# One hybrid attention and recurrence block on one core: high weights meet both token parts in one product, gate scaling on ScalarE, and two streams of work change places

## The chip, the cores and the metric

The kernel runs on one core of a Trainium2 chip. The metric is device time in microseconds (us). The kernel before takes 1622.03 us, the median of three runs between 1621.97 and 1623.56 us. Engines are named as in the profile: PE is TensorE's matmul, PEld its weight load, DVE is VectorE, ACT is ScalarE, POOL is GpSimd and SP is SyncE, which issues most DMAs.

## The reference, cut to what matters

All of it is fp32: 256 tokens and 256 context tokens of width 2048, one layer. `att`, `hgrn2_bidir`, `readout` and `rope` stand for the window attention with a sink, the gated two-way recurrence over 16 heads, its normed and gated output and the rotary embedding.

```python
mod = silu(c) @ w_ada + b_ada                       # 2048 -> 3 x 2048
shift, scale, gate = split(mod, 3)                  # the same for the context, without gate
xn = rmsnorm(x) * (1 + scale) + shift               # and cn from ctx
aq, ak, av, ag, hq, hff, hfb, hi, hg, ma, mb = split_columns(xn @ w_in)   # 19456 columns
att_branch = att(rope(aq), rope(ak), av, ctx keys and values) * silu(ag)
f = lb + (1 - lb) * sigmoid(hff)                    # forget gates, also for hfb and for the context
o = hgrn2_bidir(silu(hq), hi, 1 - f, log f, ...)    # starts from states of the context
hg_branch = readout(o) * silu(hg)                   # silu(hg): the "output gate"
y = sigmoid(ma + b0) * (hg_branch @ w_o_hgrn) + sigmoid(mb + b1) * (att_branch @ w_o_attn)
out = rmsnorm(x + gate * (y @ w_out))               # gate: "modulation's gate"
```

## The kernel before

**Split numbers.** Every large product is computed on numbers in two parts. A weight tile `raw` (128 partitions x 1024) is rounded to a high part `wh` on ACT, and DVE subtracts to get the low part `wl` (lines 76 and 77, or 597 and 598). The normed tokens and context tokens lie in `xHL` in the same two parts, transposed, 512 columns wide: 256 tokens and 256 context tokens. A product is the sum of high x high, high x low and low x high, all added up in one PSUM bank. The `raw` tiles turn over in 4 buffers, `wh` and `wl` in 3 each. A pool hands a buffer to the next load in the order of the program, and SP issues these loads in one queue.

**Stages, in order of time.** (1) Loading, transposing and modulating x, with the first forget gates. (2) Inside the block `pl("sp")`: the projection of the first value columns (`bv0`, 192 products of 512 columns, with all 512 tokens), the sums of token quarters `S` (`token_sums`, 26 DVE operations of 128x1024 and 8 ACT copies), then 13 calls of `quad_col` and 3 of `quad_tok`. (3) The recurrence, one pair of heads at a time, 8 pairs: `weave` takes the pair's chain (scans `E`, level products, states) and puts pieces of projections ("fillers": output gates 1 to 3, merge gates, attention's keys and values) between its steps on PE. (4) Projection of the recurrence's output, attention, the second projection, the last product and the norm.

**Sets of seven products.** `quad_col` and `quad_tok` are the seven-product form of a 2x2 block product: seven products of quarter blocks on combinations of weights in place of eight. `quad_col` makes 256 columns of a forget gate for all 512 tokens. It loads four quarter blocks, and `combos` makes four combinations of them on DVE (line 578: `t1`, `t2`, `b12`, `t4`). A product has 8 steps of depth; a step before has three matmuls of 256 moving columns (lines 616, 617, 621: `wh` with the high token part, `wh` with the low one, `wl` with the high one), so 24 in a product, all into one half bank. Three banks serve the seven products: banks 0 and 1 are read out after products 0, 1 and 2 (ACT copies `snap`), and the sums go on. After products 3, 4 and 5 DVE adds bank and copy into a quarter of `sg` (lines 632, 634, 636). Product 6 goes on in bank 0, so it waits until DVE has read the bank after product 4. Then ACT takes the sigmoid and DVE scales and shifts by `lbc` (line 645), and the result goes to DRAM.

**Modulation's gate.** The 2048 columns of `gate` are not made by PE: `gate_chunk` loads 256 x 512 of `w_ada` into `wg`, in the one buffer `F1`, and DVE multiplies and adds it twice into `accT` (line 198). There are 32 such chunks; after every eighth, `gate_end` transposes the sum on PE (`tqg`) and reduces it on DVE, and at the end `gcol` is turned (`tgr`, line 518) and stored. `take(gate, 2)` calls two chunks per `quad_col` and two in each half of a `quad_tok`, and `take(gate, 60)` the rest behind the last one.

**Output gate 0** (`output_gate(0)`, line 1034, 96 products of 512 columns) stands at the head of stage 3, before the query projection of the first pair.

**What sets the order.** PE's order is the order of the program in the blocks with `manual_schedule`. DVE, ACT, POOL and SP get theirs from a planner that runs over the program with priorities (`high_priority`); each engine then executes in that order and waits on semaphores. A DVE instruction that waits holds up all behind it.

Of the kernel before, what the change touches and what calls it, by code (L numbers as in the profile page):

```python
# [14 lines left out]
P = 128  # L15
# [23 lines left out]
def block_kernel(ctx: ExitStack, tc: tile.TileContext, x, c, cx, c_ctx, w_ada, b_ada, norm_gain, w_in,  # L39
# [467 lines left out]

    def gates():
# [14 lines left out]
    accT = fp.tile([P, 2, 512], F32, tag="acc", name="acc")  # L523
    gate = gates()

    with pl("sp", reuse_waits="tile") as sp:
# [74 lines left out]
        def quad_col(d, h0):  # L601
# [7 lines left out]
            snap = [None] * 2  # L609
            for (i, _, mv), src in zip(ORDER, combos(b)):  # L610
                h, lo = [a.rearrange("p (k c) -> p k c", k=8) for a in two(src)]
                z, fresh = into[i]
                for k in range(8):
                    mh, ml = mv(k)
                    o = m_[z] if len(mh.shape) == 2 else pairs_of(m_[z])
                    pe.matmul(o, h[:, k, :], mh, start=fresh and k == 0, stop=False, skip_group_check=True)  # L616
                    pe.matmul(o, h[:, k, :], ml, start=False, stop=False, skip_group_check=True)  # L617
                for k in range(8):
                    mh, ml = mv(k)
                    o = m_[z] if len(mh.shape) == 2 else pairs_of(m_[z])  # L620
                    pe.matmul(o, lo[:, k, :], mh, start=False, stop=k == 7,  # L621
                              skip_group_check=True)
                with tc.high_priority(2 * PRIO):
                    if i in (0, 1):
                        if i == 0:
                            snap[0] = base.tile([P, 512], F32, tag="bb", name="sn", bufs=2)
                        act.activation(snap[0][:, i * T: (i + 1) * T], m_[i], AF.Copy)
                    elif i == 2:
                        snap[1] = base.tile([P, 512], F32, tag="bb", name="sn", bufs=2)
                        act.activation(snap[1][:, :T], m_[0], AF.Copy)  # L630
                    elif i == 3:
                        dve.tensor_tensor(half(sg[1], 0), pairs_of(m_[1]), pairs_of(snap[1][:, :T]), op=ALU.add)
# [73 lines left out]
        with tc.manual_schedule(engines={mybir.EngineType.PE}):  # L706
# [7 lines left out]
            for g in range(2):  # L714
                token_sums(g)
# [758 lines left out]
```

## Time and profile before

| | us |
|---|---|
| median of 3 runs | 1622.03 |
| the profiled execution | 1623.79 |
| its span | 1622.0 |
| granted clock over it, as a share of full speed | 0.993 |
| PE busy / PEld busy | 1590.2 / 1374.7 |
| DVE busy / ACT busy | 1139.1 / 843.3 |
| moved by DMA | 312.86 MB, 192 GB/s |

PE is counted as busy from a matmul's start to its modelled end, and matmuls overlap, so a busy share near 98% does not say how fast they follow one another. The distance from one start to the next does, and that is what the prediction reads. In views of stages each engine has the busy us and, in brackets, its instructions; then come the granted clock, the share of the DMA engines' time and GB/s. In the list of waits a row has the total us, how often, and the longest.

### The profile page before, as it was taken

How to read it: one execution, taken by the hardware profiler on the slowest of the kernel's cores; microseconds unless marked ns; L12 is line 12 of the kernel's file. 1: busy time of each engine (PE TensorE's matmuls, PEld its weight loads, DVE VectorE, ACT ScalarE, POOL GpSimd, SP SyncE). 2: the span in 40 equal slices, each digit the busy share in tenths (PEclk: the TensorE clock that was granted, in tenths of full speed). 3: DMA queues.
4: the chain of work that ended last, by engine and by line, in shares of the span. 5: the costliest groups of instructions: out<-in, count | busy, mean ns of one | idle time of the engine just before them, and what ended most of it. 6: DMA issues, size and time to landing. Idle time of an engine off the chain costs nothing.

```text
span 1622.0 us, 28104 instructions
## 1 busy us (share of the span) xinstructions
PE 1590.2 (98%) x11250; PEld 1374.7 (85%) x11250; DVE 1139.1 (70%) x1677; ACT 843.3 (52%) x1317; POOL 87.5 (5%) x183
## 2 busy tenths in 40 slices
PE   7999899999999999999999999999999999999998
PEld 4668899999999988888888888888888888878887
DVE  4449987888887667775777877555567767656764
ACT  4334344444443346664566666443457678744442
POOL 2000000100000010110110110000000000000000
PEclk9999999999999999999999999999999999999999
DMA  9995544555554386563566566356554445467662
GB/s 370 386 366 194 164 150 132 187 172 178 187 179 160 107 273 211 183 209 124 190 221 220 186 210 196 119 180 193 184 181 138 149 130 169 155 222 244 209 197 89
DMA packets 230019, 312.86 MB, mean 193 GB/s; under 512 B 10080, under 2 KB 145664, under 8 KB 228992
## 3 DMA queue, kind: packets, MB, share of 16 engines
q1 hardware_dynamic: 216800, 266.85, 50.8%
q0 software_dynamic: 12368, 43.11, 7.5%
q8 instruction: 88, 1.44, 0.4%
q10 hardware_dynamic: 720, 1.11, 0.2%
q14 instruction: 43, 0.35, 0.1%
HBM read 290.05 MB, written 20.98 MB: 192 GB/s over the span
## 4 chain that ended last, share of the span: by engine, by line
PE 78%; issue 10%; DVE 6%; DMA 4%; ACT 1%; POOL 0%; POOLq 0%; DVEq 0%; ACTq 0%; SPq 0%
PE pj L83 14%; PE pj L85 14%; PE pj L84 14%; PE pj L141 7%; PE pj L146 4%; DMA wg<-in_w_ada_dram 2%; PE pm L616 2%; PE pm L617 2%; PE pm L621 2%; PE pj L616 2%; PE pj L617 2%; PE pj L621 2%; DMA raw<-in_w_in_dram 2%; DVE wl L598 1%; PE al L828 1%
## 5 line engine op out<-in xcount | busy, mean ns | idle before, releaser
L77 DVE TENSOR_TENSOR wl<-raw,wh 128x1024 fp32r<-128x1024 f32 x308 | 376.2, 1223 | 220.6 <-ACT wh L76 219.8
L76 ACT ACTIVATE wh<-raw 128x1024 fp32r<-128x1024 f32 x308 | 325.8, 1058 | 302.1 <-PE pj L85 213.1
L83 PE MATMUL pj<-wh,xHL 128*128 128x512 f32 (+1 forms) x832 | 322.0, 392 | 0.0
L85 PE MATMUL pj<-wh,xHL 128*128 128x512 f32 (+1 forms) x832 | 321.0, 386 | 0.0
L84 PE MATMUL pj<-wl,xHL 128*128 128x512 f32 (+1 forms) x832 | 320.6, 385 | 0.0
L85 PEld LDWEIGHTS pj<-wh,xHL 128*128 128x128 f32 x832 | 156.3, 188 | 32.0
L83 PEld LDWEIGHTS pj<-wh,xHL 128*128 128x128 f32 x832 | 156.3, 188 | 30.1 <-ACT sg L213 0.4
L84 PEld LDWEIGHTS pj<-wl,xHL 128*128 128x128 f32 x832 | 156.6, 188 | 29.6
L141 PE MATMUL pj<-xHL,wh 128*128 128x512 f32 x512 | 180.8, 395 | 0.0
L146 PE MATMUL pj<-xHL,wl 128*128 128x256 f32 x512 | 140.5, 285 | 0.0
L597 ACT ACTIVATE wh<-raw 128x1024 fp32r<-128x1024 f32 x76 | 80.3, 1058 | 93.6 <-PE pj L617 23.2
L141 PEld LDWEIGHTS pj<-xHL,wh 128*128 128x128 f32 x512 | 95.0, 188 | 18.6
L598 DVE TENSOR_TENSOR wl<-raw,wh 128x1024 fp32r<-128x1024 f32 x76 | 92.8, 1221 | 14.9 <-ACT wh L597 14.8
L84 PE MATMUL pj<-wl,bH 128*128 128x512 f32 x256 | 100.4, 393 | 0.4 <-DVE wl L77 0.4
L597 ACT ACTIVATE wh<-T 128x1024 fp32r<-128x1024 f32 x57 | 60.3, 1059 | 77.4 <-DVE T L578 27.3
L85 PE MATMUL pj<-wh,bL 128*128 128x512 f32 x256 | 99.3, 390 | 0.0
L146 PEld LDWEIGHTS pj<-xHL,wl 128*128 128x128 f32 x512 | 96.7, 189 | 2.6
L83 PE MATMUL pj<-wh,bH 128*128 128x512 f32 x256 | 91.8, 392 | 0.1
L598 DVE TENSOR_TENSOR wl<-T,wh 128x1024 fp32r<-128x1024 f32 x57 | 69.6, 1221 | 11.1 <-ACT wh L597 11.1
L874 DVE TENSOR_TENSOR A<-A,X 128x512 f32<-128x512 f32 x96 | 62.0, 688 | 9.6 <-ACT so L804 2.4
L84 PEld LDWEIGHTS pj<-wl,bH 128*128 128x128 f32 x256 | 48.1, 188 | 10.9 <-DVE wl L77 1.0
L83 PEld LDWEIGHTS pj<-wh,bH 128*128 128x128 f32 x256 | 47.8, 188 | 10.6 <-ACT bH L1067 0.5
(363 smaller groups left out, 3154.6 us busy)
## 6 DMA issues: line engine op xcount, KB each, us to landing
raw<-in_w_in_dram SPq DMA_DIRECT2D x300, 512.0 KB, 3.6
raw<-in_w_ada_dram SPq DMA_DIRECT2D x64, 512.0 KB, 8.0
wg<-in_w_ada_dram SPq DMA_DIRECT2D x32, 512.0 KB, 4.0
raw<-in_w_o_hgrn_dram SPq DMA_DIRECT2D x32, 512.0 KB, 3.5
raw<-in_w_o_attn_dram SPq DMA_DIRECT2D x32, 512.0 KB, 4.2
F<-F POOLq DMA_DIRECT2D x29, 512.0 KB, 4.4
raw<-in_w_out_dram SPq DMA_DIRECT2D x28, 512.0 KB, 4.1
v<-vo POOLq DMA_DIRECT2D x8, 512.0 KB, 5.2
```

The costliest lines, as they stand in the source:

```text
L76: act.activation(h[:, :n], raw[:, :n], AF.Copy)
L77: dve.tensor_tensor(lo[:, :n], raw[:, :n], h[:, :n].bitcast(F32), op=ALU.subtract)
L83: pe.matmul(o, s[0], m[0], start=first, stop=False)
L84: pe.matmul(o, s[0], m[1], start=False, stop=False)
L85: pe.matmul(o, s[1], m[0], start=False, stop=last)
L141: pe.matmul(banks[i].rearrange("p (a t) -> p a t", a=2), h[:, j, cs_], xHL[:, :, kt, :T], start=kt == 0, stop=kt == KT - 1)
L146: pe.matmul(banks[i][:, :T], lo[:, j, cs_], xH[:, kt, :T], start=False, stop=False)
L597: act.activation(h, src, AF.Copy)
L598: dve.tensor_tensor(lo, src, h.bitcast(F32), op=ALU.subtract)
L616: pe.matmul(o, h[:, k, :], mh, start=fresh and k == 0, stop=False, skip_group_check=True)
L617: pe.matmul(o, h[:, k, :], ml, start=False, stop=False, skip_group_check=True)
L621: pe.matmul(o, lo[:, k, :], mh, start=False, stop=k == 7, skip_group_check=True)
```

## The change

Four things change. (a) In `quad_col` a `wh` block meets both token parts in one matmul of 512 moving columns: the left half of the bank gathers high x high (and low x high), the right half high x low. The reads out of the bank are 512 wide, and DVE adds the copy to the bank and then the two halves to each other (`joined`). (b) Scaling and shifting of the forget gates go from DVE to ACT. (c) Modulation's gate is no longer computed among the seven-product sets, but in stage 3: `with_gates` calls one chunk after every `2 * STEP` moving columns of fillers. Its weights come through the common `raw` buffers. (d) Output gate 0 goes from the head of stage 3 to the place between `bv0` and the first `quad_col`, and the stores of `bv0` stand behind the token sums. `F1`, free of `wg`, holds the copies after products 0 and 1.

```diff
     def gate_chunk(acc, g, k0):
-        wr = fp.tile([P, 2, 512], F32, tag="F1", name="wg")
-        nc.sync.dma_start(wr, w_ada[k0 * P: (k0 + 2) * P, 4096 + 512 * g: 4608 + 512 * g]
-                          .rearrange("(k p) c -> p k c", p=P))
+        wr = wload(w_ada, k0 * P, 2, (4096 + 512 * g,), 512)[1][:, 0]
...
         def sums(i):
-            return lambda k: [S[:, z, i, k, :] for z in range(2)]
+            return lambda k: S[:, :, i, k, :].rearrange("p z (a t) -> p z a t", a=2)
         def sides(h, kh):
-            return lambda k: [half(X[:, 8 * kh + k, :], h) for X in (xH, xL)]
+            return lambda k: xHL[:, :, 8 * kh + k, :].rearrange("p z (a h t) -> p z a h t", a=2, h=2)[:, :, :, h, :]
...
-            m_ = [bank8()[:, :T] for _ in range(3)]
+            m_ = [bank8() for _ in range(3)]
+            s15 = fp.tile([P, 2, 512], F32, tag="F1", name="s15")
+            def joined(m, s, dst):
+                dve.tensor_tensor(s, m, s, op=ALU.add)
+                dve.tensor_tensor(dst, pairs_of(s[:, :T]), pairs_of(s[:, T:]), op=ALU.add)
...
                 for k in range(8):
-                    pe.matmul(o, h[:, k, :], mh, start=fresh and k == 0, stop=False, skip_group_check=True)
-                    pe.matmul(o, h[:, k, :], ml, start=False, stop=False, skip_group_check=True)
+                    pe.matmul(m_[z].rearrange("p (z a t) -> p z a t", z=2, a=2), h[:, k, :], mv(k),
+                              start=fresh and k == 0, stop=False, skip_group_check=True)
                 for k in range(8):
-                    pe.matmul(o, lo[:, k, :], mh, start=False, stop=k == 7,
+                    pe.matmul(pairs_of(m_[z][:, :T]), lo[:, k, :], mv(k)[:, 0], start=False, stop=k == 7,
                               skip_group_check=True)
...
-                        dve.tensor_tensor(half(sg[1], 0), pairs_of(m_[1]), pairs_of(snap[1][:, :T]), op=ALU.add)
+                        joined(m_[1], su, half(sg[1], 0))
...
-                        act.activation(half(sg[0], 1), pairs_of(m_[0]), AF.Sigmoid)
+                        act.activation(half(sg[0], 1), pairs_of(m_[0][:, T:]), AF.Copy)
+                        dve.tensor_tensor(half(sg[0], 1), pairs_of(m_[0][:, :T]), half(sg[0], 1), op=ALU.add)
...
             for i in (1, 0):
-                dve.tensor_scalar(F[:, i, :], sg[i], lbc[:, 2 + d, h0 + i: h0 + i + 1],
-                                  lbc[:, d, h0 + i: h0 + i + 1], op0=ALU.mult, op1=ALU.add)
+                act.activation(sg[i], sg[i], AF.Sigmoid)
+                act.activation(F[:, i, :], sg[i], AF.Identity, scale=lbc[:, 2 + d, h0 + i: h0 + i + 1],
+                               bias=lbc[:, d, h0 + i: h0 + i + 1])
             nc.gpsimd.dma_start(F_dr[d][h0 // 2], F.rearrange("p i t -> p (i t)"))
-            take(gate, 2)
...
             bv0 = proj_tok(w_in, C_HI, x_st, range(4))
+            for g in range(2):
+                token_sums(g)
             for t in range(2):
                 vo = fp.tile([P, 2, 512], F32, tag="F0", name="vo", bufs=2)
...
-            for g in range(2):
-                token_sums(g)
+            run(output_gate(0))
             for n in range(1, 8):
...
-            take(gate, 60)
...
+    def with_gates(filler):
+        for got in filler:
+            count[0] += got
+            if count[0] >= 2 * STEP:
+                count[0] -= 2 * STEP
+                next(gate, None)
+            yield got
...
         res = [load_forgets(0), None]
-        run(output_gate(0))
         res[1] = result(proj_col_x_g(w_in, C_HQ))
...
-            weave(pair(n // 2, n % 2, grps[n // 2], *res), inputs(n, nxt))
+            weave(pair(n // 2, n % 2, grps[n // 2], *res), with_gates(inputs(n, nxt)))
...
+    run(gate)
```

The planner's order moves with it. DVE, in the steady run of `quad_col` calls; `wl` is a low weight part, `T` and `raw` written by line 578 (586 now) are combinations, `sg` the gate's quarters, `sn` the copies. One call before:

```order
L578 TENSOR_TENSOR raw<-raw 128x1024
L632 TENSOR_TENSOR sg<-pm,sn 128x2x128
L598 TENSOR_TENSOR wl<-T,wh 128x1024
L634 TENSOR_TENSOR sg<-pm,sn 128x2x128
L598 TENSOR_TENSOR wl<-raw,wh 128x1024
L645 TENSOR_SCALAR F_2237<-sg,lbc 128x512
L636 TENSOR_TENSOR sg<-pj,sn 128x2x128
L598 TENSOR_TENSOR wl<-T,wh 128x1024
L578 TENSOR_TENSOR T<-raw,T 128x1024
L645 TENSOR_SCALAR F_2237<-sg,lbc 128x512
L598 TENSOR_TENSOR wl<-T,wh 128x1024
L578 TENSOR_TENSOR T<-raw,T 128x1024
```

and the same stretch now (`su` and `s_2058` are the 512-wide copies):

```order
L586 TENSOR_TENSOR raw<-raw 128x1024
L606 TENSOR_TENSOR wl<-T,wh 128x1024
L624 TENSOR_TENSOR sg<-su 128x2x128
L623 TENSOR_TENSOR s_2058<-pm,s_2058 128x512
L606 TENSOR_TENSOR wl<-raw,wh 128x1024
L624 TENSOR_TENSOR sg<-s_2058 128x2x128
L623 TENSOR_TENSOR s_2058<-pj,s_2058 128x512
L606 TENSOR_TENSOR wl<-T,wh 128x1024
L624 TENSOR_TENSOR sg<-s_2058 128x2x128
L586 TENSOR_TENSOR T<-raw,T 128x1024
L649 TENSOR_TENSOR sg<-pm,sg 128x2x128
L606 TENSOR_TENSOR wl<-T,wh 128x1024
```

The three single adds have become three pairs and one more add, and the two scalings by `lbc` are gone from DVE.

DVE, where pair 6 of the recurrence begins; `X` written by lines 764, 765 and 768 (770, 771, 774 now) is the scan tile `E`, which the products `tw` wait for. Before:

```order
L764 SCALAR_TENSOR_TENSOR X_10011<-F_9706,zero 128x255
L765 SCALAR_TENSOR_TENSOR X_10011<-F_9707,zero 128x255
L764 SCALAR_TENSOR_TENSOR X_10011<-F_9706,zero 128x255
L765 SCALAR_TENSOR_TENSOR X_10011<-F_9707,zero 128x255
L768 SCALAR_TENSOR_TENSOR X_10011<-F_9706,X_10011 128x512
L768 SCALAR_TENSOR_TENSOR X_10011<-F_9707,X_10011 128x512
```

and now:

```order
L770 SCALAR_TENSOR_TENSOR X_9294<-F_8969,zero 128x255
L771 SCALAR_TENSOR_TENSOR X_9294<-F_8970,zero 128x255
L783 TENSOR_TENSOR A<-qk,F_8969 128x512
L784 TENSOR_TENSOR A<-qk,F_8970 128x512
L196 SCALAR_TENSOR_TENSOR acc<-raw,cg,acc 128x512
L774 SCALAR_TENSOR_TENSOR X_9294<-F_8969,X_9294 128x512
L785 TENSOR_TENSOR qk<-A 128x512
L774 SCALAR_TENSOR_TENSOR X_9294<-F_8970,X_9294 128x512
```

Between the scans and the first `E` stand two products of the query and one gate chunk's step now, and another operation before the second.

SP's queue, in stage 3. Before, a stretch of it held weights of `w_in` alone:

```order
L66 DMA raw<-in_w_in_dram 128x4x256 x11
L66 DMA raw<-in_w_in_dram 128x2x512 x8
L66 DMA raw<-in_w_in_dram 128x4x256 x4
L66 DMA raw<-in_w_in_dram 128x2x512 x12
L66 DMA raw<-in_w_in_dram 128x4x256 x4
```

and now every fifth load, where the fillers have two token blocks, is a gate chunk's:

```order
L66 DMA raw<-in_w_in_dram 128x2x512 x4
L66 DMA raw<-in_w_ada_dram 128x2x512
L66 DMA raw<-in_w_in_dram 128x4x256 x4
L66 DMA raw<-in_w_ada_dram 128x2x512
L66 DMA raw<-in_w_in_dram 128x2x512 x4
```

The gate's loads have left the queue of the seven-product sets, where each waited for the one buffer `F1`.

More of the change, by code (lines that the diff above doesn't have):

```diff
@@ L506, in pairs_of, with run, output_gate @@
         return a.rearrange("p (a t) -> p a t", a=2)
+    def run(g):
+        for _ in g:
+            pass
+    def output_gate(g):
+        bg = yield from proj_tok_g(w_in, C_HG + 512 * g, x_st, range(2))
+        for t in range(2):
+            sg = base.tile([P, 512], F32, tag="sm", name="sgg", bufs=3)
+            act.activation(sg, bg[t], AF.Sigmoid)
+            dve.tensor_tensor(sg, bg[t], sg, op=ALU.mult)
+            nc.gpsimd.dma_start(hg_dr[g][:, t * 512: (t + 1) * 512], sg)
     def gates():
@@ L521, in gates @@
         nc.gpsimd.dma_start(gate_rows, grow_[:KT, :P])
-    accT = fp.tile([P, 2, 512], F32, tag="acc", name="acc")
-    gate = gates()
     with pl("sp", reuse_waits="tile") as sp:
@@ L618, in quad_col @@
                 for k in range(8):
-                    mh, ml = mv(k)
-                    o = m_[z] if len(mh.shape) == 2 else pairs_of(m_[z])
-                    pe.matmul(o, lo[:, k, :], mh, start=False, stop=k == 7,
+                    pe.matmul(pairs_of(m_[z][:, :T]), lo[:, k, :], mv(k)[:, 0], start=False, stop=k == 7,
                               skip_group_check=True)
                 with tc.high_priority(2 * PRIO):
[L624 to L627, printed above, removed]
+                    if i < 2:
+                        act.activation(s15[:, i, :], m_[i], AF.Copy)
@@ L628, in quad_col @@
                     elif i == 2:
[L629 to L630 removed]
+                        su = base.tile([P, 512], F32, tag="bb", name="su", bufs=2)
+                        act.activation(su, m_[0], AF.Copy)
                     elif i == 3:
[L632 removed]
+                        joined(m_[1], su, half(sg[1], 0))
@@ L633, in quad_col @@
                     elif i == 4:
-                        dve.tensor_tensor(half(sg[1], 1), pairs_of(m_[0]), pairs_of(snap[0][:, T:]), op=ALU.add)
+                        joined(m_[0], s15[:, 1, :], half(sg[1], 1))
                     elif i == 5:
-                        dve.tensor_tensor(half(sg[0], 0), pairs_of(m_[2]), pairs_of(snap[0][:, :T]), op=ALU.add)
+                        joined(m_[2], s15[:, 0, :], half(sg[0], 0))
                     else:
-                        act.activation(half(sg[0], 1), pairs_of(m_[0]), AF.Sigmoid)
@@ L691, in quad_tok @@
                     for k in range(4):
-                        sh, sl = [a if len(a.shape) == 3 else pairs_of(a) for a in st_(4 * s + k)]
+                        sh, sl = [st_(4 * s + k)[:, z] for z in range(2)]
                         for z in range(2):
@@ L701, in quad_tok @@
                         done_with(i)
-                take(gate, 2)
             for t in range(2):
@@ L997, in block_kernel @@
     done = []
-    def run(g):
-        for _ in g:
-            pass
     STEP = 24 * 512
@@ L1032, in load_gate @@
         nc.gpsimd.dma_start(grp[2].rearrange("p t c -> p (t c)"), hg_dr[g])
-    def output_gate(g):
-        bg = yield from proj_tok_g(w_in, C_HG + 512 * g, x_st, range(2))
-        for t in range(2):
-            sg = base.tile([P, 512], F32, tag="sm", name="sgg", bufs=3)
-            act.activation(sg, bg[t], AF.Sigmoid)
-            dve.tensor_tensor(sg, bg[t], sg, op=ALU.mult)
-            nc.gpsimd.dma_start(hg_dr[g][:, t * 512: (t + 1) * 512], sg)
     def merge_out(row, n):
@@ L1130, in block_kernel @@
     with tc.manual_schedule(engines={mybir.EngineType.PE}):
+        accT = fp.tile([P, 2, 512], F32, tag="acc", name="acc")
+        gate, count = gates(), [0]
         grps = [[None] * 3 for _ in range(4)]
         res = [load_forgets(0), None]
-        run(output_gate(0))
         res[1] = result(proj_col_x_g(w_in, C_HQ))
```

8 lines of the change are left out of this document (1 added, 7 removed).

## The prediction

> **What bounds the kernel now.** I read the page first, then a table of busy time by stage, then the list of PE's waits, then single rows.
>
> ```profile
> PE 1590.2 (98%) x11250; PEld 1374.7 (85%) x11250; DVE 1139.1 (70%) x1677; ACT 843.3 (52%) x1317; POOL 87.5 (5%) x183
> ```
>
> PE has work nearly always, so time goes only if PE needs less time for a stage or waits less in it. The stages that the change touches (the run of `quad_col`, the run of `quad_tok`, the recurrence), and three short stretches:
>
> ```profile
> 176.50:450.50 274.00, 267.53 (x2192) 265.97 (x2192) 229.17 (x260) 125.34 (x170) 10.93 (x16) 0.99 0.54 168
> 450.50:580.50 130.00, 125.96 (x1022) 125.34 (x1021) 101.23 (x108) 48.29 (x51) 7.15 (x17) 0.97 0.48 157
> 611.00:1062.00 451.00, 448.68 (x4264) 380.70 (x4263) 327.07 (x551) 280.26 (x523) 44.95 (x101) 1.00 0.58 186
> ...
> 186.90:193.70 6.80, 6.21 (x29) 6.21 (x30) 6.47 (x7) 3.88 (x5) 0.00 (x0) 0.50 0.46 138
> 500.90:504.30 3.40, 3.40 (x18) 3.40 (x18) 2.55 (x3) 0.73 (x1) 0.00 (x0) 0.50 0.66 199
> 538.50:541.90 3.40, 3.40 (x17) 3.40 (x17) 2.45 (x2) 0.42 (x2) 0.51 (x1) 0.50 0.18 68
> ```
>
> The reader is to see two things: DVE is the second engine everywhere (84%, 78% and 73% of the three stages), and the first two stages hold three stretches at half the clock (0.50). PE's waits, by line:
>
> ```profile
> PE pj L616 <- ACT wh L597: 3.0, 2, 2.2
> PE tw L893 <- DVE X L768: 2.3, 4, 0.6
> PE pj L697 <- DVE wl L598: 1.9, 1, 1.9
> ...
> PE tgr L518 <- DVE gcol L208: 1.4, 1, 1.4
> PE pj L621 <- DVE wl L598: 1.3, 1, 1.3
> PE pj L616 <- DVE sg L634: 1.3, 2, 0.7
> ...
> PE tqg L204 <- DVE vo L657: 0.8, 1, 0.8
> PE tqg L204 <- ACT sg L638: 0.5, 1, 0.5
> ```
>
> All but `tw` lie between 176 and 580 us. In the recurrence PE waits 2.3 us in all: it is full there, with DVE as the cover.
>
> **The joined product (A).** Distances between starts count. From the chain of waits (the `wl` matmuls of two products in a row) and the timeline of PE:
>
> ```profile
> 212.79 0.96 PE pj L621 x8
> 215.67 0.96 PE pm L621 x8
> ```
>
> ```profile
> 149.80 0.39 PE L84 MATMUL pj<-wl,xHL 128*128 128x512 f32 x1
> ...
> 176.54 0.39 PE L85 MATMUL pj<-wh,xHL 128*128 128x512 f32 x1
> ...
> 604.35 0.40 PE L141 MATMUL pj<-xHL,wh 128*128 128x512 f32 x1
> 604.59 0.28 PE L146 MATMUL pj<-xHL,wl 128*128 128x256 f32 x1
> 604.71 0.40 PE L141 MATMUL pj<-xHL,wh 128*128 128x512 f32 x1
> ```
>
> A product of 24 matmuls of 256 columns takes 2.88 us, 0.120 each. 118 steps of 512 columns lie between 149.80 and 176.54: 0.2266 each, which is 13 ns less than two of 256. Line 141 already reads both token parts in one matmul, and with its 256-column partner takes 0.36, no more than 0.2266 + 0.120 within the row's rounding. Now a product is 8 x 0.2266 + 8 x 0.120 = 2.77 us, 0.107 less; 13 calls of 7 products make 91, so **-9.7 us**. Operands cut into more pieces than line 141's have no row; bounds: no loss, or all of the gain lost.
>
> The Trainium skill, page TensorE: Matmul & The Clock Gate, section Back-to-back issue gap, gives columns / 2.4 GHz plus some 2.5 ns for an isolated matmul. By it two of 256 cost 2.5 ns more than one of 512, and 728 pairs would save an estimated 1.8 us, not 9.7. The rows above do not agree with it here (13 ns), and they decide.
>
> **What the seven-product sets need of DVE and ACT (D).**
>
> ```profile
> L598 DVE TENSOR_TENSOR wl<-raw,wh 128x1024 fp32r<-128x1024 f32 x75 | 91.6, 1221 | 14.9 <-ACT wh L597 14.8
> L578 DVE TENSOR_TENSOR T<-raw,T 128x1024 f32<-128x1024 f32 x38 | 46.5, 1223 | 0.8
> L198 DVE SCALAR_TENSOR_TENSOR acc<-wg,cg,acc 128x512 f32<-128x512 f32 x53 | 39.7, 749 | 13.9 <-DMA wg<-in_w_ada_dram 13.6
> L645 DVE TENSOR_SCALAR F<-sg,lbc 128x512 f32<-128x512 f32 x26 | 14.1, 543 | 1.9 <-ACT sg L638 1.9
> L657 DVE TENSOR_TENSOR sn<-pj,sn 128x512 f32<-128x512 f32 x5 | 3.5, 691 | 0.6 <-PE pj L698 0.6
> L636 DVE TENSOR_TENSOR sg<-pj,sn 128x256 f32<-128x256 f32 x7 | 3.0, 422 | 2.3 <-PE pj L621 2.3
> ```
>
> ```profile
> L597 ACT ACTIVATE wh<-raw 128x1024 fp32r<-128x1024 f32 x75 | 79.3, 1058 | 93.6 <-PE pj L617 23.2 <-PE pj L698 20.3 <-PE pm L617 19.8
> L640 ACT ACTIVATE sg<-sg 128x512 f32<-128x512 f32 x13 | 8.2, 633 | 20.7 <-DVE sg L634 20.7
> ```
>
> DVE in a call before: 11 x 1.222 + 3 x 0.422 + 2 x 0.543 = 15.8 us, with four gate steps 18.8, of PE's 20.2. Now 11 x 1.222 + 3 x (0.691 + 0.422) + 0.422 = 17.2 of 19.4. ACT gains two scalings (0.63 as a bound, from line 640) and wider copies, 2.1 us more than 10 a call: hidden behind PE's 19.4, and 28 us over 13 calls if it were not. Nobody waits for the gates' store until stage 3. Line 623 keeps bank 0 for 0.69 instead of 0.42 before product 6, covered by product 5's 2.77; uncovered it is 13 x 0.27 = 3.5 us. What may bind instead is loading:
>
> ```profile
> DVE T L578 <- DMA raw<-in_w_in_dram: 17.0, 15, 1.9
> DVE acc L198 <- DMA wg<-in_w_ada_dram: 13.6, 16, 1.8
> ```
>
> `t1` of the next call already waits 1.1 us for its block, since the `raw` buffer comes free late. PE's call shrinks by 0.75, the load does not. Bounds: 0, or A given back (9.7); the wait lies in DVE's slack of 2.2 us now, so nearer to nothing: **+1.5**.
>
> **The start of the sets (B).** PE waits 3.0 + 1.3 us at 180 to 187 us, since DVE is still at the token sums when the first `quad_col` stands there, and then 6.80 us at half clock hold 29 matmuls, worth 29 x 0.120 = 3.5 us; 0.6 of the waits lie in that stretch. Together 4.3 - 0.6 + 3.3 = 7.0. Now 96 x 0.2266 = 21.8 us of output gate stand between, and no gate steps on DVE: the 26 sums and 8 low parts of `bv0` are 34 x 1.22 = 41.5 us against 43.5 (192 x 0.2266) of PE for `bv0` alone. **-6.5**, between -4 and -7.
>
> **Stalls from gate chunks (C).** The longest later wait shows its cause in the timelines, first DVE's and then PE's (time, length, instruction, and the wait ahead of it in square brackets):
>
> ```profile
> 496.71 1.54 DVE L198 SCALAR_TENSOR_TENSOR acc<-wg,cg,acc 128x512 f32<-128x512 f32 x2 [1.76 <-DMA wg<-in_w_ada_dram]
> ```
>
> ```profile
> 499.44 0.38 PE L697 MATMUL pj<-wl,S 128*128 128x256 f32 x1 [1.89 <-DVE wl L598]
> ```
>
> DVE stood 1.76 us before a gate step whose load had not come, and behind it `wl` was late for PE. This 1.9, the waits of `tqg` and `tgr` (0.8 + 0.5 + 1.4) and line 616 on line 634 (1.3) make 5.9; the two stretches of 3.4 us at half clock hold 18 and 17 matmuls, worth 2.1 each, so 2.6 more. Of 8.5 I take **-7.8**: only the 1.3 has no sure tie to the chunks (low bound 5).
>
> **What stage 3 pays (E).** 64 gate steps of 0.749 are 48 us, and DVE goes from 327 to 375 of 451 us (83%). Most lie in its idle time; a chunk holds one of four `raw` buffers, and four pieces of filler at 12 x 0.2266 = 2.7 us are 11 us between its loads. In front of a step that waits for its load, `wl` of the fillers would stand behind it, and PE behind that. By the order three places are on the path. (1) At pair 6 two products and one gate step stand before the first `E`, 0.69 + 0.69 + 0.75 = 2.1, and one more operation before the second, 0.7; at pair 4 one step and one operation, 1.4; PE already waits there (`tw`): 4.0, if DVE had nothing else to wait for. (2) The third `gate_end` uses the bank that `ob` needs next: four transposes and a reduction, about 1.2, from the 1.4 that `tgr` waited. (3) The first pair loses output gate 0 as cover:
>
> ```profile
> 580.34 0.40 PE L83 MATMUL pj<-wh,xHL 128*128 128x512 f32 x1
> ```
>
> ```profile
> 585.66 0.54 POOL L1089 DMA_DIRECT2D F<-F  x1 [3.51 <-DMA v<-vo]
> ```
>
> ```profile
> 591.45 0.69 DVE L764 TENSOR_TENSOR_SCAN X<-F,zero 128x255 f32<-128x255 f32 x1 [3.12 <-DMA F<-F]
> ...
> 594.35 0.68 DVE L768 SCALAR_TENSOR_TENSOR X<-F,X 128x512 f32<-128x512 f32 x1
> ```
>
> From the end of the sets (580.34) to `E` it takes 14.7 us, by stores and loads on POOL's queue. Cover is now 32 x (0.2266 + 0.120) + 2.7 = 13.8, and a gate step stands before line 774 too: 1.3. Together **+6.5**; bounds 0.5 (the filler order gives slack at the pairs) and 48 (all steps on the path).
>
> In the trace the clock fell to 0.50 some 1.5 us behind the wait of 1.9 that ends at 499.44, so a wait of 3 us at pair 6 may cost more here. The Trainium skill, page TensorE: Matmul & The Clock Gate, section What's actually happening, has the clock fall only after an idle window of some 3.4 us; by that no wait here would change it, and the trace does not agree. A stretch like the ones above costs 1.3 us; I leave it in the bounds.
>
> **The sum.** -9.7 - 6.5 - 7.8 + 1.5 + 6.5 = -16.0. The profiled execution took 1623.79 (span 1622.0 and 1.8 around it), so 1607.8; the median of the runs is 1.8 lower, so **1606 us**. Its own range: A kept, B -7 to -5, C -8.5 to -6, D 0 to 4, E 2.5 to 11 give 1599 to 1616.
>
> **The rivals.** *Stage 3 hides it all* (E 0.5, D 0): 1606 - 6 - 1.5 = 1598.5. For it: DVE idles 124 us there; against: PE already waits for `E`. Chance 0.20. *The sets become bound by loading or DVE*: a call stays at 20.16, A goes, 1606 + 8.2 = 1614. For it: the 1.1 us waits for `raw`; against: calls without gate steps run at 7 x 2.88 with no wait of PE. Chance 0.12. *The 2.5 ns rule*: A is 1.8, 1614 as well, against the rows: 0.02. *Slower*: gate steps sit on the pairs' chain of DVE, price up to 48; without E the sum is -22.5, so it decides once 22.5 of the 48, 30 of 64 steps, show on PE; two thirds give 1606 - 6.5 + 32 = 1632. For it: planned order puts steps into the chain at two pairs; against: at the others they stand behind it. Chance 0.06. My forecast has 0.60.
>
> **Range and chances.** 1597 to 1617 holds the forecast, both cases at 1614 and most of the one at 1598.5. A measurement of this kernel tells 0.2%, 3.2 us, from no change. Faster 0.91 (all but the slower rival and the upper tail), the same 0.04, slower 0.05.
>
> **What would show it.** A: eight matmuls of 512 start 0.227 apart in line 624's place, and 2.77 us from product to product; 13 calls in some 255 us instead of 274. B: no wait and no half clock before the first call. C: no `acc` among DVE's waits in the sets. D: the wait of `t1` for `raw` about 1 us. E: waits of `tw` grow from 2.3 to some 6 us, with DVE's `E` as their end. I am wrong if a call stays near 20.2 us, or if fillers wait for `wl` behind `acc` in stage 3.

## The result, and the profile after

The changed kernel takes 1629.71 us, the median of seven runs (1625.55 to 1630.81), against 1622.03 before: a ratio of 1.0042, with a 95% interval from 1.003 to 1.0055. It is slower by 0.4%; 1606 us, 1% faster, was predicted, with 1597 to 1617 as the range. The profiled execution took 1626.34 us (span 1624.6), 2.6 more than the profiled one of before. The medians are 7.7 apart, so the stages below show the loss at its low end; where the other executions lose some 5 us more is not on record. Executions of one kernel spread by up to 12 us, and each table of stages shows one of them, up to 5.4 us from its kernel's median.

The first view is again the page, and then busy time by stage (the run of `quad_col`, the run of `quad_tok`, the main part of the recurrence):

```profile
PE 1584.1 (98%) x10522; PEld 1335.9 (82%) x10522; DVE 1151.7 (71%) x1703; ACT 873.0 (54%) x1343; POOL 84.9 (5%) x183
```

```profile
198.60:452.80 254.20, 254.20 (x1458) 223.73 (x1457) 210.45 (x236) 151.80 (x193) 7.50 (x14) 1.00 0.45 136
452.80:573.80 121.00, 121.00 (x1011) 121.00 (x1010) 90.22 (x88) 49.41 (x52) 7.16 (x17) 1.00 0.43 140
611.00:1064.00 453.00, 435.22 (x4160) 366.63 (x4159) 348.47 (x592) 265.76 (x501) 45.78 (x103) 0.98 0.65 211
```

The sets have become perfect for PE: its busy time is the whole length of both stages, at full clock. The recurrence has not: PE's busy time was 448.7 of 451 before and is 435 of 453 now, and the clock is 0.98. PE's waits from the end of the sets to the end of the recurrence:

```profile
PE tw L899 <- DVE X L774: 16.7, 8, 3.4
PE pj L84 <- DVE wl L77: 1.3, 1, 1.3
PE ob L975 <- DVE X L961: 1.0, 1, 1.0
PE ob L973 <- DVE redg L204: 0.9, 1, 0.9
PE to L993 <- DVE redg L204: 0.8, 1, 0.8
```

Six of the eight pairs wait for `E` (`X`, line 774) now, two of them twice, 16.7 us in all instead of 2.3 at four pairs. Counted from 0, the waits are 3.1 us at pair 0, 2.6 at pair 1, 2.4 at pair 4, 3.4 at pair 5, 3.5 at pair 6 and 1.6 at pair 7. None of the waits of before in the sets is left.

The stages can be laid side by side by the start of the first matmul in each (PE's timeline of either profiled execution). In this table, and in the ones of the experiments, "to E" goes from the end of `quad_tok` to the first `tw` product, which needs the first `E`; "pairs" from there to the last product of a pair (`to`); "rest" from there to the last matmul of the kernel.

| us | beginning | `bv0`, output gate 0 | `quad_col` | `quad_tok` | to E | pairs | rest |
|---|---|---|---|---|---|---|---|
| before | 133.1 | 43.7 | 274.3 | 129.2 | 35.8 | 458.4 | 539.4 |
| changed | 133.2 | 65.4 | 254.2 | 121.0 | 17.3 | 485.4 | 539.8 |
| difference | +0.1 | +21.7 | -20.1 | -8.2 | -18.5 | +27.0 | +0.4 |

Output gate 0 is 21.7 us of PE, which moved from "to E" to the stage of `bv0`. Without it the sets gave 28.3 us, more than the 22.5 predicted for them, and the recurrence took 30.2 back, where 6.5 had been predicted.

How a gate chunk makes `E` late is seen in DVE's timeline ahead of the pair with the longest wait (pair 5), and PE's beside it:

```profile
881.93 0.75 DVE L196 SCALAR_TENSOR_TENSOR acc<-raw,cg,acc 128x512 f32<-128x512 f32 x1 [1.40 <-DMA raw<-in_w_ada_dram]
882.60 0.42 DVE L156 TENSOR_TENSOR hsum<-pj,hsum 128x256 f32<-128x256 f32 x1
882.93 0.74 DVE L196 SCALAR_TENSOR_TENSOR acc<-raw,cg,acc 128x512 f32<-128x512 f32 x1
883.59 1.22 DVE L77 TENSOR_TENSOR wl<-raw,wh 128x1024 fp32r<-128x1024 f32 x1
...
885.40 0.68 DVE L770 TENSOR_TENSOR_SCAN X<-F,zero 128x255 f32<-128x255 f32 x1
...
887.73 1.27 DVE L774 SCALAR_TENSOR_TENSOR X<-F,X 128x512 f32<-128x512 f32 x2
```

```profile
884.66 0.39 PE L85 MATMUL pj<-wh,xHL 128*128 128x512 f32 x1
888.45 1.97 PE L899 MATMUL tw<-cs,X 128*128 128x128 f32 x8 [3.41 <-DVE X L774]
...
891.93 0.63 PE L84 MATMUL pj<-wl,xHL 128*128 128x512 f32 x1
892.35 0.63 PE L85 MATMUL pj<-wh,xHL 128*128 128x512 f32 x1
```

DVE stands 1.40 us before a gate step whose load has not landed; behind it, in DVE's fixed order, come a sum, the second step, `wl`, and only then the scans and `E`. PE has run out of fillers at 885 and stands until 888.45. In the kernel before, DVE was early at pair 5: it stood 1.28 us before the last `wl` of the fillers, and PE waited 0.58 us for `E`.

```profile
895.11 1.23 DVE L77 TENSOR_TENSOR wl<-raw,wh 128x1024 fp32r<-128x1024 f32 x1 [1.28 <-ACT wh L76]
...
899.26 1.27 DVE L768 SCALAR_TENSOR_TENSOR X<-F,X 128x512 f32<-128x512 f32 x2
```

At pairs 1 to 7 this idle time was 1.28 to 1.57 us before; now it is gone at all but pairs 2 and 3, and those two are the ones that do not wait for `E`.

When PE goes on at 888.45, its matmuls of 512 columns come to start 0.43 us apart, not 0.227. The row of that stretch shows why (its length, busy time by engine, and the granted clock, 0.50):

```profile
887.40:894.10 6.70, 5.65 (x18) 4.78 (x19) 5.91 (x12) 1.19 (x2) 0.00 (x0) 0.50 0.25 72
```

The clock stands at half for 6.7 us. Between 580 and 1066 us there are five stretches of 3.4 us at half clock (from 590.4, 829.3, 887.3 with its follower, and 952.2), each worth up to 1.7 us; before, there was none in the recurrence. So a late `E` can be paid twice: by the wait, and by the slow matmuls after it. Of the 27.0 us that the pairs grew by, 15.5 are more idle time of PE and 7.1 matmuls at half clock, by the distances between starts; the likely rest are the transposes of the gate's sums, which took 3.2 us in the sets before.

### The profile page after: what moved, and what is told of

It reads as the page before. It is cut to its first block, busy times and chain, and to the rows that moved or that the text cites. A ratio compares the mean times of both kernels' runs of the same rounds, so it can differ in the third digit from the quotient of the medians.

```text
span 1624.6 us, 26679 instructions
## 1 busy us (share of the span) xinstructions
PE 1584.1 (98%) x10522; PEld 1335.9 (82%) x10522; DVE 1151.7 (71%) x1703; ACT 873.0 (54%) x1343; POOL 84.9 (5%) x183
## 4 chain that ended last, share of the span: by engine, by line
PE 87%; DVE 6%; DMA 3%; issue 2%; ACT 1%; POOL 0%; POOLq 0%; DVEq 0%; ACTq 0%
PE pj L83 13%; PE pj L84 13%; PE pj L85 13%; PE pj L141 6%; PE pj L630 5%; PE pm L630 5%; PE pj L146 3%; DMA raw<-in_w_ada_dram 3%; PE pj L633 3%; PE pm L633 3%; PE pj L415 2%; PE pa L311 2%; DVE wl L77 2%; PE pj L705 1%; PE pj L704 1%
## 5 line engine op out<-in xcount | busy, mean ns | idle before, releaser
L196 DVE SCALAR_TENSOR_TENSOR acc<-raw,cg,acc 128x512 f32<-128x512 f32 x60 | 44.8, 747 | 31.0 <-DMA raw<-in_w_ada_dram 30.9
L84 PEld LDWEIGHTS pj<-wl,bH 128*128 128x128 f32 x256 | 48.1, 188 | 10.8 <-DVE wl L77 1.0
```

The costliest lines, as they stand in the source:

```text
L84: pe.matmul(o, s[0], m[1], start=False, stop=False)
```

## The experiments

Each changes the changed kernel in one thing, unless it says otherwise. Two theories on the recurrence stood at the beginning. One: the gate's steps take DVE's time ahead of `E`. Two: their loads hold DVE up, and take weight buffers from the fillers.

**The recurrence without the gate.** Neither loads nor steps nor the transposes of the sums:

```diff
-        for g in range(4):
-            for k0 in range(0, KT, 2):
-                gate_chunk(accT[:, 0, :], g, k0)
-                yield
-            gate_end(accT[:, 0, :], g)
         yield
...
-                next(gate, None)
+                pass
```

> The changed kernel with modulation's gate left out (no loads of its weights, no steps, no transposes of its sums; the gate rows are the bias alone). It gives the price of the gate in the recurrence. The changed kernel's stage from the end of the sets to the last turn took 502.4 us against 472.1 before. If the gate is the cause of the 30.2 us, as both theories below say, this stage falls to 473 to 480 (the first pair still has lost output gate 0 as cover) and the time to 1599 to 1607. If it stays above 1615, the cause is another part of the change: the lost cover, or the new place of the stores.

It took 1612.53 us, ratio to the kernel before 0.9942 (0.992 to 0.9963), higher than expected, but for a reason ahead of the change: in the profile the beginning took 143.1 us instead of 133.2, since the first weights came at 352 GB/s instead of 386 (stages from 40 to 100 us). The stages from there on are as expected:

| us | beginning | `bv0`, gate 0 | `quad_col` | `quad_tok` | to E | pairs | rest |
|---|---|---|---|---|---|---|---|
| no gate | 143.1 | 65.4 | 255.2 | 121.0 | 16.9 | 460.1 | 540.4 |
| steps, no loads | 133.8 | 65.4 | 254.2 | 121.0 | 16.9 | 472.2 | 540.0 |
| loads, tiny steps | 132.7 | 65.4 | 256.1 | 121.0 | 17.0 | 467.9 | 539.9 |

The pairs come back to 460.1: the gate is the cause of 25.3 of their 27.0 us. "To E" does not come back: that part is the lost cover.

**Steps without loads, and loads with tiny steps.**

```diff
-        wr = wload(w_ada, k0 * P, 2, (4096 + 512 * g,), 512)[1][:, 0]
+        wr = cs[:, 0:512].unsqueeze(1).to_broadcast([P, 2, 512])
```

> The changed kernel with the gate's 64 steps on DVE kept, but on a constant tile that lies in SBUF, so nothing is loaded for them and no weight buffer is held (the gate's product with its weights is left out). Theory 1, the steps' own time: 45 to 48 us of DVE in front of E decide, since E stood at the edge at four pairs before; then it stays near the changed kernel, 1618 to 1630. Theory 2, the loads: a step that waits for its load holds up all DVE work behind it (31 us of such waits in the stage), and its load takes one of four buffers from the fillers; then it falls to 1600 to 1610.

```diff
     def gate_chunk(acc, g, k0):
+        acc = acc[:, 0:8]
...
-                dve.scalar_tensor_tensor(acc, wr[:, j, :], cc, acc, op0=ALU.mult, op1=ALU.add)
+                dve.scalar_tensor_tensor(acc, wr[:, j, 0:8], cc, acc, op0=ALU.mult, op1=ALU.add)
```

> The changed kernel with the gate's loads and waits kept, but each step works on 8 of the 512 columns (the other columns of the gate are left out), so DVE has about 40 us less to do. Theory 1, the steps' own time: the waits of PE for E fall from 16.7 us to some 3, and the time to 1600 to 1608. Theory 2, the loads: the waits for the gate's loads stay at about 30 us, PE's waits for E above 10, and the time at 1616 to 1630.

Steps alone took 1612.79 us (0.9943, 0.9923 to 0.9962), loads alone 1610.33 (0.993, 0.9912 to 0.9948): leaving out either the loads or the steps' length saved 17 to 19 us of the changed kernel's time, so neither theory holds by itself. Against no gate the pairs grew by 12.1 with steps alone and by 7.8 with loads alone; with both it is 25.3, which is 5.4 more than the sum. PE's waits for `E` in the three, and DVE's waits for the loads with tiny steps:

```profile
PE tw L894 <- DVE X L769: 5.1, 5, 2.7
```

```profile
PE tw L899 <- DVE X L774: 9.8, 7, 3.0
```

```profile
PE tw L900 <- DVE X L775: 8.6, 6, 2.9
```

```profile
DVE acc L197 <- DMA raw<-in_w_ada_dram: 28.7, 22, 5.7
```

(no gate, steps alone, loads alone, and the last of loads alone). DVE stood 28.7 us for the loads, nearly the 30.9 of the changed kernel, and PE lost only 7.8: a DVE with little else to do catches up. Half-clock stretches between 580 and 1066 us: one without gate, three with steps, one with loads, five with both. The two stretches above the sum are up to 3.4 of the 5.4; some 2 us were not resolved. The changed kernel's profiled execution lies 3.4 us below its median, those of the other three within 1 of theirs, so the excess over the sum may be larger.

**Chunks earlier in the pair.** Four in each pair after every 1.5 units of fillers, none in the last 2.5:

```diff
+        count, left = 0, 4
         for got in filler:
-            count[0] += got
-            if count[0] >= 2 * STEP:
-                count[0] -= 2 * STEP
+            count += got
+            if left and count >= 3 * STEP // 2:
+                count -= 3 * STEP // 2
+                left -= 1
                 next(gate, None)
```

> The changed kernel with the same 32 chunks in the recurrence, but four in each pair after every 1.5 instead of 2 units of fillers, so that none is called in the last 2.5 units before the next pair's scans. Under both theories what decides is which gate work stands on DVE ahead of E: the waits of PE for E fall from 16.7 us to 3 to 6, with the half clock behind them gone, so 1603 to 1613. If DVE is simply too full in the stage, or the four weight buffers too few, wherever the chunks stand, PE waits elsewhere (for wl) and the time stays above 1620.

1627.79 us, 1.0029 (1.0014 to 1.0043); the pairs took 491.6. The second case: the waits for `E` fell to 5.5, and others took their place (PE's waits in the recurrence):

```profile
PE pj L84 <- DVE wl L77: 11.9, 3, 5.7
PE tw L899 <- DVE X L774: 5.5, 4, 3.1
PE ob L975 <- DVE X L961: 5.0, 3, 3.8
```

The same places once with steps only and once with loads only tell what failed (the edits are those shown above):

> The version with four early chunks in each pair, its steps on a constant tile and no loads (the gate's product with its weights left out). If the steps cost PE because they stand on DVE ahead of E, early steps without loads cost next to nothing: from the first E to the last turn 458 to 463 us, against 472 for late steps without loads. If DVE has no room for them wherever they stand, 470 to 476.

> The version with four early chunks in each pair, its loads and waits kept and each step on 8 of 512 columns (the rest of the gate left out). If what made that version as slow as the changed kernel (491.6 us from the first E to the last turn) is the loads, four in 6 instead of 8 units of fillers on four shared buffers, this takes 475 to 490, more than the 468 of the same loads at the later places. If it is the steps' time, 460 to 468.

They took 1614.54 and 1610.19 us in one execution each. The pairs took 473.9 with early steps alone and 468.9 with early loads alone, next to nothing different from the late places (472.2 and 467.9). So an earlier place in the pair made neither price lower: with both, what no longer delayed `E` delayed `wl` or the levels behind.

**The joined product alone undone**, in the same banks:

```diff
-                    pe.matmul(m_[z].rearrange("p (z a t) -> p z a t", z=2, a=2), h[:, k, :], mv(k),
-                              start=fresh and k == 0, stop=False, skip_group_check=True)
+                    for y_ in range(2):
+                        pe.matmul(pairs_of(m_[z][:, y_ * T: (y_ + 1) * T]), h[:, k, :], mv(k)[:, y_],
+                                  start=fresh and k == 0 and y_ == 0, stop=False, skip_group_check=True)
```

> The changed kernel with only the joined matmul undone: high weights meet the two token parts in two matmuls of 256 columns, into the same two halves of the bank; all adds, copies and places as in the changed kernel. The trace after has 230 ns from start to start for the joined matmul (90% of them between 226 and 236) and 119 for its partner, so 2.793 us for a product against 2.88 before; by that the 13 calls grow by 91 x 0.087 = 7.9 us, to 20.16 each, and the time by as much. By the 13 ns of the prediction it would be 9.7; if the 256-column form were only 2.5 ns dearer a pair, 1.8; if the calls were bound by DVE (17.2 a call) or by loads, nothing.

1639.03 us, 1.01 (1.0084 to 1.0115). `quad_col` took 262.1 us instead of 254.2 and every other stage stayed within 1.3 us: 7.9, as the trace after had said. (The medians are 9.3 apart, too coarse to tell 7.9 from the predicted 9.7.) Rows from the chain of waits of the changed kernel and of this one show a product of each:

```profile
201.53 1.84 PE pj L630 x8
203.37 0.95 PE pj L633 x8
204.32 1.84 PE pj L630 x8
```

```profile
202.40 1.92 PE pj L631 x16
204.32 0.96 PE pj L634 x8
205.28 1.92 PE pj L631 x16
```

2.79 us against 2.88.

**Scaling of the forget gates back on DVE.**

```diff
-                act.activation(F[:, i, :], sg[i], AF.Identity, scale=lbc[:, 2 + d, h0 + i: h0 + i + 1],
-                               bias=lbc[:, d, h0 + i: h0 + i + 1])
+                dve.tensor_scalar(F[:, i, :], sg[i], lbc[:, 2 + d, h0 + i: h0 + i + 1],
+                                  lbc[:, d, h0 + i: h0 + i + 1], op0=ALU.mult, op1=ALU.add)
```

> The changed kernel with only the scaling and shifting of the forget gates back on DVE (2 x 0.54 us a call). By the prediction DVE has 2.2 us of slack in a call of 19.4 and goes to 18.3: quad_col stays at 254.2 us (13 calls of 19.55) and the time within 3 us of the changed kernel, 1627 to 1633. If DVE sets the pace of the calls, as the version with the gate in the sets suggests (21.3 us a call with 1.5 x 2 us more on DVE), the calls grow by up to 1.1 us each, 14 in all: 1636 to 1645.

1634.42 us, 1.0072 (1.0052 to 1.0091), between the two forecasts, and `quad_col` 261.2: half of the second theory's growth, 0.54 us a call. The medians differ by 4.7 us, less than the 7.0 of this stage. Busy time in `quad_col`, and PE's waits in the sets:

```profile
198.60:459.80 261.20, 256.72 (x1458) 224.33 (x1458) 218.97 (x258) 132.40 (x168) 7.50 (x14) 1.00 0.43 132
```

```profile
PE pm L630 <- DVE s L623: 1.6, 2, 0.8
PE pj L630 <- DVE s L623: 1.4, 2, 0.8
PE pm L630 <- ACT wh L605: 0.9, 4, 0.3
```

DVE is busy for 84% of the stage and holds PE up all the same, at the banks' sums (line 623) and behind ACT.

**Output gate 0 back at the head of the recurrence.**

```diff
-            run(output_gate(0))
             for n in range(1, 8):
...
         res = [load_forgets(0), None]
+        run(output_gate(0))
```

> The changed kernel with only output gate 0 put back to the head of the recurrence. By the prediction the sets lose 6.5 again at their start (waits for the token sums and half clock) and the first pair gets back 1.3 of cover: 5 us slower than the changed kernel. By the trace after, the first pair's products wait 3.3 us for E with some 1.5 of half clock behind, so the pair gets back 4 to 5 and the kernel is 1.5 to 3 slower. The stretch from the first product of bv0 to the first turn of E says which, without the rest of the recurrence.

1627.32 us, 1.0029 (1.0018 to 1.0039): 2.4 faster than the changed kernel by the medians. The two intervals overlap, so the sign is not sure, but neither forecast came true. The sets begin without any wait here too; from the first product of `bv0` to the first `E` it takes 454.8 us, against 457.8. In these two executions the move of output gate 0 did nothing for the sets, and cost the first pair 3.

**The gate back among the sets**, and **partly so**:

```diff
             nc.gpsimd.dma_start(F_dr[d][h0 // 2], F.rearrange("p i t -> p (i t)"))
+            take(2)
...
                     if s == 1:
                         done_with(i)
+                take(2)
...
                 quad_tok(C_HI + 512 * g, v_dr[g])
+            take(60)
```

> The changed kernel with modulation's gate back among the sets (two chunks a call of quad_col, two in each half of quad_tok, the rest behind), its weights through the common raw buffers; joined products, ScalarE's scaling and output gate 0 as changed. By the prediction's terms the sets lose 7.8 again by stalls and the recurrence gains 6.5: 1 us slower than the changed kernel, 1630. By the trace after (30 us more in the recurrence, of which 25 with the gate) the recurrence gains about 25 and the sets lose 5 to 10: 1606 to 1613, so faster than both kernels.

> The changed kernel with one chunk of the gate in each call of quad_col, two in each half of quad_tok, 25 in all, and the last 7 in the recurrence as in the changed kernel (in its first two pairs). If a chunk costs by the DVE time and loads around it, one in a call finds room (DVE 17.2 + 1.5 of 19.5 us) and the sets lose no more than 3; 7 chunks of 32 in the recurrence cost 7/32 of 25, some 5: 1604 to 1612, near the version with all of them in the sets. If a chunk stalls a call whatever room there is, no better than that version by more than 3.

| us | beginning | `bv0`, gate 0 | `quad_col` | `quad_tok` | to E | pairs | rest | median |
|---|---|---|---|---|---|---|---|---|
| all in the sets | 133.8 | 65.4 | 277.4 | 128.2 | 17.0 | 460.1 | 539.6 | 1632.85 |
| 25 in the sets, 7 in the pairs | 132.7 | 65.4 | 268.1 | 129.3 | 17.3 | 467.8 | 540.0 | 1626.14 |

Ratios 1.0067 (1.0052 to 1.0082) and 1.0028 (1.0016 to 1.0041). Both forecasts of all in the sets missed: the pairs gave back the 25 us, but the sets lost 30.4, not 5 to 10. The mixed version missed too, with one chunk in a call costing 1.07 us (13.9 in 13 calls) where it was to find room. With the gate among them the sets take 405.6 us, more than the 403.5 of before: all the changes together bring nothing there. Which of them loses what the joined product gains was not separated; the gate's weights come through `raw` here, and through `F1` before. Busy time of the two stages and the largest waits of PE in them, with all chunks in the sets:

```profile
199.20:476.30 277.10, 261.18 (x1466) 227.86 (x1465) 239.40 (x285) 151.62 (x193) 8.80 (x16) 0.99 0.56 169
476.60:604.80 128.20, 124.18 (x1016) 123.16 (x1015) 102.91 (x109) 49.40 (x53) 7.66 (x18) 0.99 0.52 165
```

```profile
PE tqg L202 <- DVE sg L656: 4.9, 1, 4.9
PE pm L637 <- DVE s L630: 4.4, 3, 2.0
PE pm L637 <- ACT wh L612: 2.3, 1, 2.3
PE pm L637 <- DVE redg L204: 2.0, 1, 2.0
```

DVE has 18.4 us of work in a call of 21.3, and PE waits for it.

**A third home: the projection behind the recurrence.** Output gate 0 is at the head of the recurrence here, one or two chunks stand in each pair, and the others beside the weight blocks of `w_o_hgrn` (24 chunks; the version with 16 has `u % 2 == 1`, and two chunks in a pair after 3 units each):

```diff
+        count, left = 0, 1
...
+            if left and count >= 4 * STEP:
+                count = 0
+                left -= 1
                 next(gate, None)
...
-        by = proj_tok(w_oh, n * 512, b_st, range(2))
+        g, by = proj_tok_g(w_oh, n * 512, b_st, range(2)), None
+        for u in range(8):
+            next(g)
+            if u % 4 != 3:
+                next(gate, None)
+        by = result(g)
```

> Output gate 0 at the head of the recurrence as before the change, joined products and ScalarE's scaling as changed, and the gate's 32 chunks in a third place: one in each of the 8 pairs (after 4 units of fillers) and 24 in the projection of the recurrence's output behind it (three to every four weight blocks), where no chain of scans stands behind a step: DVE is busy for 45.7 of 88 us there, the DMA engines 0.59. Theory 1, chunks cost where a chain without slack stands behind them on DVE (E in the recurrence, a full DVE in the sets): 24 are hidden there, 8 cost at most 8/32 of 25, so 1604 to 1613, faster than both kernels. Theory 2, a chunk costs 0.8 to 1 us of PE wherever it stands, as in the sets and the recurrence (30 and 25 us for 32): 1622 to 1630.

> As the version with 24 chunks behind the recurrence, but 16 there (one to every two weight blocks) and two in each pair (after 3 and 6 units of fillers). Theory 1: the 16 in the pairs cost 16/32 of 25 at most, 12 us, less where they lie far from E: 1606 to 1619, and slower than with 24 by some 0 to 6. Theory 2 (0.8 to 1 us for each, anywhere): the same as with 24 within 3 us, 1622 to 1630.

| us | beginning | `bv0` | `quad_col` | `quad_tok` | to E | pairs | rest | median |
|---|---|---|---|---|---|---|---|---|
| 8 in pairs, 24 behind | 132.7 | 43.7 | 254.3 | 121.0 | 35.8 | 455.9 | 577.5 | 1631.59 |
| 16 in pairs, 16 behind | 133.2 | 43.7 | 255.0 | 121.0 | 36.6 | 464.2 | 560.8 | 1621.35 |

Ratios 1.0051 (1.0036 to 1.0066) and 0.9994 (0.9985 to 1.0003). Neither theory was right: one chunk in a pair costs nothing that shows (455.9, where the kernel before has 458.4), two cost some 6, but in the projection 16 cost 21 and 24 cost 38. The four waits for `E` of 0.6 us stayed as they were in the kernel before, with one chunk as with two:

```profile
PE tw L898 <- DVE X L773: 2.3, 4, 0.6
```

In the projection the weights come late (ACT's waits with 24 chunks, 1060 to 1170 us):

```profile
ACT wh L76 <- DMA raw<-in_w_o_hgrn_dram: 55.4, 23, 5.0
```

ACT waits for weights 23 times. In the same stretch SP's queue stood 55.5 us until a `wl` and 21.3 us until a gate step had freed one of the four buffers, so the chunks' share of them is the likely cause; the DMA engines were also busier, 0.77 against 0.60 before, and no run separates the two.

**What the prices point to.** Output gate 0 at the head of the recurrence, 12 chunks in `quad_tok` (two in each half), 16 in the pairs (two in each), 4 in the projection (`u == 3`). In this version and the last two the copy ahead of the sink's load reads `cols` in place of `gcol`, which is late there:

```diff
                     if s == 1:
                         done_with(i)
+                for _ in range(2):
+                    next(gate, None)
...
+        count, left = 0, 2
...
+            if left and count >= 3 * STEP:
```

> The parts that the runs found cheap, together: joined products, ScalarE's scaling, output gate 0 at the head of the recurrence; the gate's 32 chunks spread: 12 in quad_tok (two in each half), 16 in the pairs (two in each, after 3 and 6 units of fillers), 4 in the projection behind. Theory, from the stages of the runs: sets 43.7 + 254.3 + 129 (8 for the twelve), to the first E 36, pairs 464, and 543 to the last matmul behind 133 of the beginning, so 1603 where the kernel before has 1614 at this point: 11 faster, 1608 to 1616. Rival: chunks cost about the same, 0.8 us each, wherever they stand (26 for 32), and only the joined product, ScalarE's scaling and the calls' freedom remain: 1617 to 1623.

| us | beginning | `bv0` | `quad_col` | `quad_tok` | to E | pairs | rest | median |
|---|---|---|---|---|---|---|---|---|
| 12 + 16 + 4 | 132.7 | 43.7 | 254.7 | 124.0 | 35.9 | 467.3 | 540.4 | 1603.34 |

1603.34 us (1600.60 to 1608.73), 0.9873 (0.9857 to 0.989): 1.3% faster than the kernel before, and faster than was expected, so this forecast missed too; the table shows the execution of 1608.73 us. PE's waits from `bv0` to the projection's end:

```profile
PE pj L84 <- DVE wl L77: 4.2, 2, 2.8
PE tw L903 <- DVE X L778: 2.3, 4, 0.6
PE pm L707 <- DVE wl L609: 1.5, 2, 1.3
```

`tw` is back at the 2.3 of before. Twelve chunks in `quad_tok` cost 3.0 here, and 8.3 in the mixed version, where 13 more stand in `quad_col` in front of them; four in the projection cost 1.0. A last version, with 18 chunks in `quad_tok`, one in each pair and 6 behind, was forecast at 1597 to 1602 and has no time: its order ends in a deadlock.

## Why the prediction was wrong

**What failed is the step on stage 3 (E).** +6.5 was predicted, from three places, and 30.2 came: 27.0 in the pairs and 3.2 before the first `E`. (By the prediction's own terms its first place adds up to 4.2, not 4.0, and its third to 1.6, not 1.3; that decides nothing.)

The prediction counted the gate steps that the order puts between the last fillers and `E`, at pairs 4 and 6. There it was near: 4.0 on top of the waits of before, 1.2, and 5.9 came. At the other pairs it priced the steps at nothing: "at the others they stand behind it", and "Most lie in its idle time" (124 us of DVE in the stage). That is what failed. The traces point to the idle time of DVE just ahead of the chain, 1.28 to 1.57 us a pair before. Four chunks a pair, with their waits for loads, used it up at most pairs, and pairs 1, 5 and 7 waited 7.6 us in all, of which the kernel before had 1.2. Other products behind the chain waited 4.3 us more. The half clock, up to 8.5 us in five stretches, had been left "in the bounds" as 1.3 at one place. The runs confirm the gate as the cause of 25.3 of the 27.0, and that neither its steps nor its loads alone are the price. The idle time elsewhere in a pair could not be used either: steps alone cost 12 to 14 us wherever they stood.

The range took E up to 11 only, though its own bound was 48. The slower rival (gate steps on the pairs' chain) named the mechanism in part, and had 0.06. That its "two thirds" of 48 is 32, and 30 came, is luck: no reason was given for two thirds, and steps alone cost 12; the rest is loads, half clock and lost cover. Its point of decision, 22.5, was too low by the sets' greater gain: in the profiled executions it lies at 27.8 (28.3 less 0.5 in the beginning and the rest), and the 30.2 are just above.

**A, the joined product:** -9.7 predicted, -7.9 measured twice (254.2 against 262.1 us, and 91 products by 2.793 instead of 2.88). The mechanism and its hiding were right. The mis-sized term is the step of 512 columns (line 630): 230 ns on average with the operand in pieces (90% between 226 and 236), not 226.6. Line 141's rows had it: 0.36 for a pair is more than 0.2266 + 0.120 = 0.347, and was taken for rounding; over 448 such pairs in the kernel before, its 512 columns take 233 ns. That the pieces are the reason was not tried by itself.

**B and C, the gate's stalls in the sets, and D:** -6.5 - 7.8 + 1.5 = -12.8 predicted; the sets gave 28.3 - 7.9 = 20.4. By the distances between starts, PE had lost 20.5 us in the sets before: 10.8 in waits, 5.5 at half clock, 3.2 in the transposes of the gate's sums and 1.0 in delays of less than 0.15 us each. The prediction had nearly all of the first two and none of the last two, shaved 1.2 off B and C, and took 1.5 off for D. For B it named two reasons, output gate 0 in between and no gate steps on DVE. The first was not needed: with output gate 0 back in its place the start has no wait either. The second fits: in the kernel before, DVE did ten gate steps between 147 and 182 us, among the token sums. The later place of `bv0`'s stores, changed in the same edit, was not tried by itself. D, the loads of the calls, cost nothing measurable: PE is busy for the whole of the stage.

**ScalarE's scaling** was costed at nothing, as DVE had 2.2 us of slack in a call. Undone, it costs 7.0 us in `quad_col`. With DVE busy for 16.8 us in a call of 20.1 (218.97 us in 13 calls of 261.2) it already holds PE up at single banks; the average slack was no cover.

**Output gate 0:** 1.3 predicted for the lost cover, 3.2 measured, with a stretch of half clock at its end (from 590.4). By the run that undoes it, this part of the change is a loss of 2 to 3 us by itself.

On the clock, the prediction weighed a rule of the Trainium skill (page TensorE: Matmul & The Clock Gate, section What's actually happening): a fall to half after an idle window of some 3.4 us. The stretches in the sets and the recurrence last 3.41 or 6.83 us, one or two times its window. PE had been idle for about 2.3 us when the clock fell at 887.3, so a whole idle window is not needed here; and a wait of 2.6 us that ended at 649.5 had no stretch behind it, so the length of a wait alone does not tell.

## What to carry to other kernels

Work that is moved "into idle time" of an in-order engine has a price that grows with its density: over the eight pairs of heads one chunk in each cost nothing that shows, two 6 to 9 us, four 25 to 32 (one profiled execution each, good to some 5 us). So ask for each stage how much fits before its chain has to wait, and spread the work over several stages. Doing so, with output gate 0 back in its place, turned a change that lost 0.4% into one that gains 1.3%, with the same joined product; output gate 0 alone is 2.4 of the 26 us between the two. Look for the room in the engine's idle time just ahead of the chain (1.3 us a pair here), not in that of the whole stage (124 us). The small waits at the chain's end do not tell it: the 2.3 us of `tw` were the same with none, one and two chunks in each pair.

## What the runs showed of the hardware

The matmul of 512 columns in line 630, whose moving operand comes in several pieces, starts its follower after 230 ns on average; those of `bv0`, with the operand in one run, after 226.6. A half-clock stretch of 3.4 us near a wait costs PE up to 1.7 us on top of the wait. And the same beginning took 133.2 us in one kernel and 143.1 in another that differs only later, with its weights at 386 and 352 GB/s; what made the difference stays open.
